# A row of 1/rms for 256 tokens: two small transfers by way of DRAM in place of a product with diagonals

## The chip, the cores and the metric

The kernel runs on one core of one Trainium2 chip. The metric is the device time of one execution in microseconds (us), lower is better. Five engines matter here: PE (TensorE, with its weight loads shown as PEld), DVE (VectorE), ACT (ScalarE), POOL (GpSimd) and SP (SyncE, which only issues transfers). Each works through its own list of instructions in order and waits on semaphores for the others; transfers run on 16 DMA engines.

## The reference

A decoder trunk of two layers on 256 tokens of width 1024, all float32. Each layer norms its input, multiplies it with a wide input projection, runs two attention-like branches, and ends in an MLP. The part that the change touches is the first norm of a layer and what is scaled by it:

```python
def rmsnorm(x, gain):
    y = xf * lax.rsqrt(jnp.mean(xf * xf, axis=-1, keepdims=True) + NORM_EPS)
    return (y * gain).astype(x.dtype)

for l in range(DEPTH):                       # DEPTH = 2
    h = rmsnorm(x, g_mix[l])
    proj = jnp.matmul(h, w_in[l])            # 256 x 1024 times 1024 x 9216
    q_r, k_r, v_r, g_r, q_s, k_s, v_s, gate_a, gate_b = jnp.split(proj, splits, axis=-1)
    ...                                      # rotary + retention, stick-breaking attention, gates
    x = x + jnp.matmul(merged, w_out[l])
    h = rmsnorm(x, g_mlp[l])
    x = x + jnp.matmul(jnp.square(jax.nn.relu(jnp.matmul(h, w_up[l]))), w_down[l])
return rmsnorm(x, g_final)
```

## The kernel before, in words

**The product stream.** All weights go through one stream of units (512 x 512 floats, 1 MB each, loaded on SP's queue, L62). Each unit is cut into two halves of 2 x 128 rows. `_split` (L67) turns a half into a high part `whi` (a cast on ACT, L75) and a low part `wlo` (a subtraction on DVE, L78), and PE multiplies the high and low parts with high and low parts of the activations. `raw` has 3 buffers, `whi` and `wlo` have 4 each, and `ahead` (L86) splits three halves ahead of the one that PE takes. A call of `cols512` (L368) does four halves, that is 512 output columns; after each half it calls a `tick` function, in which work of other kinds is slipped in. `half_T` and `half_W` give the product with the columns on the partitions and the tokens along the free axis; `half_N` the other way round.

**The norm.** The gain is multiplied into the activations ahead of the product, the factor 1/rms of each token only behind it. `Norm.rstd` (L299) adds the sums of squares on DVE and calls `rstd_col` (L230), which ends in a power on POOL (L235) and gives a column `r`: 128 partitions x 2, one value per token. That column serves the products whose tokens lie on partitions. Where the tokens lie along the free axis (the q of the stick-breaking branch, and both rotary tables), the same 256 values are needed as a row on all 128 partitions: `rb`, 128 x 256.

**How the row is made before.** `diagonals` (L238) scales the identity with the two columns of `r` on DVE (two instructions, tile `dg`); `rstd_rows` (L246) multiplies a matrix of ones with `dg` on PE (tile `bc`, in a PSUM bank of pool psA) and copies the bank to `rb` on DVE.

**Where it stands.** `norm_tick` (L420) runs after each of the first eight halves of a layer. Halves 0 to 3 make the first 512 columns of q, halves 4 to 7 the second. The column `r` and the diagonals come at tick 3 in layer 0 and tick 4 in layer 1, the product of the row at tick 5 with the scaled tables `cr` and `sr` (L441, L442), and `evac` at tick 6: it multiplies the first 512 columns of q with `rb` (L460), splits them, and so gives back their PSUM banks. In layer 0 `columns(1)` follows: a small transposition of the second gains on PE (tile `gps`, also a bank of psA), copied by ACT into `gcol` (L191). A scheduler puts the instructions of each engine in order from these places, so an instruction can stand some places ahead of or behind where it is written; only those in `keep_in_program_order` stay as written.

**Banks.** psA has four banks, given out in turn. Halves 8 to 11 (the first 512 columns of k) need all four, so in layer 0 they need the banks of the first q columns and of `gps` free.

Of the kernel before, what the change touches and what calls it, by code (L numbers as in the profile page):

```python
# [11 lines left out]
F32 = mybir.dt.float32  # L12
# [3 lines left out]
ALU = mybir.AluOpType  # L16
PSUM = bass.MemoryType.PSUM

P = 128
D = 1024  # L20
S = 256
# [79 lines left out]
def kernel(ctx, tc, x, w_in, p_ret, p_sb, w_out, w_up, w_down, g_mix, g_mlp, g_final,  # L101
                      c_sq, c_tab, c_decay, out):
    nc = tc.nc
# [4 lines left out]
    lo_pool = ctx.enter_context(tc.tile_pool(name="lo", bufs=4))  # L108
    wk = ctx.enter_context(tc.tile_pool(name="wk", bufs=2))
    small = ctx.enter_context(tc.tile_pool(name="small", bufs=2))  # L110
    psA = ctx.enter_context(tc.tile_pool(name="psA", bufs=4, space=PSUM))
    psB = ctx.enter_context(tc.tile_pool(name="psB", bufs=4, space=PSUM))

# [29 lines left out]
    ident = const.tile([P, P], F32, name="ident")  # L143
# [19 lines left out]
    tri_f, ones = cst[:, 0, :], cst[:, 1, :]  # L163
# [3 lines left out]
    def load_constants():  # L167
        nc.sync.dma_start(out=gn[1], in_=g_mlp.rearrange("l (k p) -> (l k) p", p=P))
        nc.sync.dma_start(out=cst, in_=c_sq[:, 1:3, :])
        nc.sync.dma_start(out=tab, in_=c_tab)  # L170
        nc.sync.dma_start(out=dec, in_=c_decay)
# [15 lines left out]
    def columns(i):  # L187

        gps = psA.tile([P, 512], F32, tag="a", name="gps")
        nc.tensor.transpose(gps[:, :16], gn[i], ident[0:16, 0:16])  # L190
        nc.scalar.copy(out=gcol[:, 16 * i:16 * i + 16], in_=gps[:, :16])  # L191
# [43 lines left out]
        nc.gpsimd.tensor_tensor(out=r[:, :n], in0=v[:, :n], in1=half[:, :n], op=ALU.pow)  # L235
        return r

    def diagonals(r):  # L238

        dg = wk.tile([P, 768], F32, tag="z", name="dg")[:, 0:S]  # L240
        for t in range(2):
            tc.keep_in_program_order(
                nc.vector.tensor_scalar(dg[:, t * P:(t + 1) * P], ident, r[:, t:t + 1], None, ALU.mult))
        return dg

    def rstd_rows(dg):  # L246

        bc = psA.tile([P, 512], F32, tag="a", name="bc")
        nc.tensor.matmul(bc[:, :S], lhsT=ones, rhs=dg, start=True, stop=True)
        rb = wk.tile([P, S], F32, tag="rb", name="rb", bufs=1)  # L250
        nc.vector.tensor_copy(out=rb, in_=bc[:, :S])
        return rb

    class Norm:
# [160 lines left out]
    def mix(l, norm):  # L415
        h = norm.h
        state = {"n": 0}


        def norm_tick():  # L420
            state["n"] += 1
            if l == 0 and state["n"] == 1:
                load_constants()
            if l == 0 and state["n"] <= 3:
                for i in ((0,), (1, 2), (3,))[state["n"] - 1]:
                    tc.keep_in_program_order(norm.square(*divmod(i, 2)))
            if state["n"] == (3 if l == 0 else 4):
                state["rc"] = norm.rstd()
                state["dg"] = diagonals(state["rc"])
            if state["n"] == 4:  # L430
                if l == 0:
                    tc.keep_in_program_order(nc.vector.tensor_copy(out=trir, in_=tri_f))
                    tc.keep_in_program_order(nc.vector.tensor_copy(out=onesr, in_=ones))
            if state["n"] == 5:
                rc = state["rc"]
                rb = rstd_rows(state["dg"])
                rcs = small.tile([P, 2], F32, tag="rcs", name="rcs")
                nc.vector.tensor_scalar(rcs, rc[:, 0:2], P ** -0.5, None, ALU.mult)
                cr = wk.tile([P, S], F32, tag="cr", name="cr", bufs=1)
                sr = wk.tile([P, S], F32, tag="sr", name="sr", bufs=1)  # L440
                nc.vector.tensor_tensor(out=cr, in0=tab[:, 0, :], in1=rb, op=ALU.mult)  # L441
                nc.vector.tensor_tensor(out=sr, in0=tab[:, 1, :], in1=rb, op=ALU.mult)  # L442
                state.update(rb=rb, rcs=rcs, cr=cr, sr=sr)
            if state["n"] == 6:
                state["evac"]()
                if l == 0:
                    columns(1)
# [29 lines left out]
        if l == 0:  # L477
            pairs0 = cols512(half_T, h, norm_tick)
        else:
            pairs0 = halves(cols512(half_W, h, norm_tick, four(psA, "a")))  # L480
        state["evac"] = lambda: evac_q(0, pairs0)
        evac_q(1, halves(cols512(half_W, h, norm_tick, four(psB, "b"))))
        rc, rb, rcs = state["rc"], state["rb"], state["rcs"]
        for c in range(2):
# [364 lines left out]
```

## Time and profile before

| | |
|---|---|
| Time, median of 3 runs | 905.8 us (905.64 to 905.99) |
| The profiled execution's own time | 906.1 us |
| Its span (first to last instruction) | 904.4 us |
| Granted TensorE clock | 1.00 throughout |
| PE busy | 896.4 us, 99% of the span |
| DVE busy | 616.3 us, 68% |
| ACT busy | 532.3 us, 59% |
| POOL busy | 12.2 us, 1% |
| 16 DMA engines, weight queue | 55.0% of the span, 161.89 MB |

How to read it: a busy share is an average over the whole span, so a small edit is read from the stage in which it stands. Layer 0's stage is the first 35 us of the span, layer 1's the stretch from 450 to 480 us. The chain that ended last tells which engine's work set the end; an idle time in a timeline stands in brackets with what ended it. Times within a timeline are microseconds from the span's start.

### The profile page before, as it was taken

To read this page: it belongs to the slowest core of one execution; us is meant where nothing else is said; L and a number is where in the kernel's file an instruction comes from. 1 tells how busy PE (TensorE), PEld (TensorE's weight loads), DVE (VectorE), ACT (ScalarE), POOL (GpSimd) and SP (SyncE) were. 2 spreads that over 40 slices of the span, in tenths; PEclk is the share of its full clock that TensorE was granted. 3 is DMA by queue.
4 is the path that set the end of the run, shared out by engine and by line. 5 is a ranking of instruction groups with operands and counts; after the bars stand their busy time and mean duration, and the time that the engine had idled before them with its cause. 6 is when DMAs were issued, how large, how long until landed. Compare 5 with 4: busy or idle time off the path is not lost.

```text
span 904.4 us, 11880 instructions
## 1 busy us (share of the span) xinstructions
PE 896.4 (99%) x4608; PEld 762.5 (84%) x4608; DVE 616.3 (68%) x829; ACT 532.3 (59%) x760; POOL 12.2 (1%) x20
## 2 busy tenths in 40 slices
PE   9999999999999999999999999999999999999997
PEld 7888888888888888888888888888888888888886
DVE  5865995775666666666676579857756666666665
ACT  5755688544456555555656566875444574646472
POOL 0000000000000000000000000000000000000000
PEclk9999999999999999999999999999999999999999
DMA  9755454545555655555555654544555655565641
GB/s 328 232 186 186 140 187 140 186 140 186 187 187 179 193 187 186 187 190 185 192 179 189 194 177 149 178 155 153 170 197 187 186 187 186 186 190 188 202 165 47
DMA packets 82151, 163.83 MB, mean 181 GB/s; under 512 B 2704, under 2 KB 3120, under 8 KB 82096
## 3 DMA queue, kind: packets, MB, share of 16 engines
q1 hardware_dynamic: 81488, 161.89, 55.0%
q10 hardware_dynamic: 608, 1.19, 0.4%
q8 instruction: 36, 0.59, 0.3%
q14 instruction: 19, 0.16, 0.1%
HBM read 162.02 MB, written 1.05 MB: 180 GB/s over the span
## 4 chain that ended last, share of the span: by engine, by line
PE 99%; DMA 1%; ACT 0%; DVE 0%; POOLq 0%; issue 0%; ACTq 0%
PE pa L356 18%; PE pa L358 18%; PE pa L357 18%; PE pb L333 12%; PE pa L333 11%; PE pb L337 6%; PE pa L337 5%; PE tp L225 1%; PE pa L319 1%; PE rop L636 1%; PE pb L356 1%; PE pb L358 1%; PE pb L357 1%; PE op L562 1%; PE z L518 1%; DMA x<-in_x_dram 1%
## 5 line engine op out<-in xcount | busy, mean ns | idle before, releaser
L78 DVE TENSOR_TENSOR wlo<-raw,whi 128x1024 fp32r<-128x1024 f32 (+1 forms) x306 | 371.5, 1216 | 234.4 <-ACT whi L75 231.2
L75 ACT CAST whi<-raw 128x1024 fp32r<-128x1024 f32 (+1 forms) x305 | 318.3, 1046 | 296.6 <-PE pa L357 195.4
L333 PE MATMUL pb<-h,whi 128*128 128x512 f32 x448 | 141.2, 396 | 0.0
L333 PE MATMUL pa<-h,whi 128*128 128x512 f32 x416 | 131.0, 396 | 0.0
L356 PE MATMUL pa<-whi,h 128*128 128x512 f32 x288 | 114.3, 397 | 0.0
L358 PE MATMUL pa<-wlo,h 128*128 128x512 f32 x288 | 112.4, 390 | 0.0
L357 PE MATMUL pa<-whi,h 128*128 128x512 f32 x288 | 112.2, 390 | 0.0
L337 PEld LDWEIGHTS pb<-h,wlo 128*128 128x128 f32 x448 | 84.1, 188 | 20.0 <-DVE wlo L78 0.2
L337 PEld LDWEIGHTS pa<-h,wlo 128*128 128x128 f32 x416 | 78.1, 188 | 18.4
L356 PE MATMUL pa<-whi,up 128*128 128x512 f32 x240 | 93.5, 390 | 0.0
L357 PE MATMUL pa<-whi,up 128*128 128x512 f32 x240 | 93.4, 389 | 0.0
L358 PE MATMUL pa<-wlo,up 128*128 128x512 f32 x240 | 93.4, 389 | 0.0
L337 PE MATMUL pb<-h,wlo 128*128 128x256 f32 x448 | 88.0, 278 | 0.0
L337 PE MATMUL pa<-h,wlo 128*128 128x256 f32 x416 | 81.8, 278 | 0.0
L333 PEld LDWEIGHTS pb<-h,whi 128*128 128x128 f32 x448 | 68.5, 189 | 0.3
L333 PEld LDWEIGHTS pa<-h,whi 128*128 128x128 f32 x416 | 64.0, 189 | 0.7
L358 PEld LDWEIGHTS pa<-wlo,h 128*128 128x128 f32 x288 | 54.1, 188 | 11.8
L357 PEld LDWEIGHTS pa<-whi,h 128*128 128x128 f32 x288 | 54.2, 188 | 10.2
L356 PEld LDWEIGHTS pa<-whi,h 128*128 128x128 f32 x288 | 54.2, 188 | 10.1
L358 PEld LDWEIGHTS pa<-wlo,up 128*128 128x128 f32 x240 | 45.0, 188 | 9.4
L356 PEld LDWEIGHTS pa<-whi,up 128*128 128x128 f32 x240 | 45.0, 188 | 9.0
L357 PEld LDWEIGHTS pa<-whi,up 128*128 128x128 f32 x240 | 45.0, 188 | 9.0
(177 smaller groups left out, 1139.8 us busy)
## 6 DMA issues: line engine op xcount, KB each, us to landing
raw<-in_w_in_dram SPq DMA_DIRECT2D x62, 1024.0 KB, 5.2
raw<-in_w_up_dram SPq DMA_DIRECT2D x32, 1024.0 KB, 5.4
raw<-in_w_down_dram SPq DMA_DIRECT2D x32, 1024.0 KB, 5.0
raw<-in_p_sb_dram SPq DMA_DIRECT2D x8, 1024.0 KB, 5.1
raw<-in_p_ret_dram SPq DMA_DIRECT2D x8, 1024.0 KB, 5.1
raw<-in_w_out_dram SPq DMA_DIRECT2D x8, 1024.0 KB, 5.1
raw<-in_w_in_dram SPq DMA_DIRECT2D x3, 512.0 KB, 6.7
x<-in_x_dram SPq DMA_DIRECT2D x3, 256.0 KB, 6.6
```

The costliest lines, as they stand in the source:

```text
L75: m = self.nc.scalar.copy(out=hi[:, sl], in_=src[:, sl])
L78: m = self.nc.vector.tensor_tensor(out=lo[:, sl], in0=src[:, sl], in1=hi[:, sl].bitcast(F32), op=ALU.subtract)
L225: m = nc.tensor.transpose(tp[:, a * S + t * P:a * S + (t + 1) * P], src(t)[:, f:f + P], ident)
L319: nc.tensor.matmul(banks[o // 2][:, (o % 2) * S:(o % 2 + 1) * S], lhsT=w[:, kk, o * P:(o + 1) * P], rhs=a, start=first and kk == 0 and n = ...
L333: nc.tensor.matmul(banks[o], lhsT=whi[:, kk, o * P:(o + 1) * P], rhs=a.rearrange("p a b -> p (a b)"), start=first and kk == 0, stop=False, ...
L337: nc.tensor.matmul(banks[o][:, S:2 * S], lhsT=wlo[:, kk, o * P:(o + 1) * P], rhs=act[(k0 + kk) // 2][:, kk, 0, :], start=False, stop=last ...
L356: nc.tensor.matmul(banks[t], lhsT=ahi, rhs=whi[:, kk, :], start=st, stop=False)
L357: nc.tensor.matmul(banks[t], lhsT=alo, rhs=whi[:, kk, :], start=False, stop=False)
L358: nc.tensor.matmul(banks[t], lhsT=ahi, rhs=wlo[:, kk, :], start=False, stop=sp)
L518: nc.tensor.matmul(z0[:, j * S:(j + 1) * S], lhsT=k0[c][:, a, r + j, :], rhs=part(qs, 2 * i + j, b), start=(n == 0 and j == 0), stop=(n == ...
L562: nc.tensor.matmul(op[:, o:o + S], lhsT=v0[c][:, a, e], rhs=wp[:, j, b, :], start=(n == 0 and j == 0), stop=False, skip_group_check=True)
L636: nc.tensor.matmul(op[:, o:o + S], lhsT=sc[:, i, a:b], rhs=vr[hd][:, t, j, :], start=(n == 0 and a == 0), stop=(n == 2 and t == 1), skip_g ...
```

## The change

The diagonals, the product with ones and the copy from PSUM go away. In their place POOL issues two transfers as soon as it has made `r`: the 128 x 2 column is written to a 1 KB buffer in DRAM (token order, so each of the 256 values is a run of its own), and that buffer is read back into `rb` once for each of the 128 partitions. The second waits for the first. `cr`, `sr` and `evac` move to tick 7 in layer 0 and tick 8 in layer 1.

```diff
+    dram = ctx.enter_context(tc.tile_pool(name="dram", bufs=2, space=bass.MemoryType.DRAM))
...
-    def diagonals(r):
-        dg = wk.tile([P, 768], F32, tag="z", name="dg")[:, 0:S]
-        for t in range(2):
-            tc.keep_in_program_order(
-                nc.vector.tensor_scalar(dg[:, t * P:(t + 1) * P], ident, r[:, t:t + 1], None, ALU.mult))
-        return dg
-    def rstd_rows(dg):
-        bc = psA.tile([P, 512], F32, tag="a", name="bc")
-        nc.tensor.matmul(bc[:, :S], lhsT=ones, rhs=dg, start=True, stop=True)
+    def rows(r):
+        row = dram.tile([2, P], F32, tag="row", name="row")
+        nc.gpsimd.dma_start(out=row.rearrange("t p -> p t"), in_=r[:, 0:2])
         rb = wk.tile([P, S], F32, tag="rb", name="rb", bufs=1)
-        nc.vector.tensor_copy(out=rb, in_=bc[:, :S])
+        nc.gpsimd.dma_start(out=rb, in_=row.rearrange("t p -> (t p)").partition_broadcast(P))
         return rb
...
             if state["n"] == (3 if l == 0 else 4):
                 state["rc"] = norm.rstd()
-                state["dg"] = diagonals(state["rc"])
+                state["rb"] = rows(state["rc"])
...
-            if state["n"] == 5:
-                rc = state["rc"]
-                rb = rstd_rows(state["dg"])
+            if state["n"] == (7 if l == 0 else 8):
+                rc, rb = state["rc"], state["rb"]
...
-            if state["n"] == 6:
                 state["evac"]()
                 if l == 0:
                     columns(1)
```

How the order moves, at three places. In the rows, the number behind `whi` or `wlo` is the half of the stream (0 to 151 are layer 0, 152 onwards layer 1, so 157 is half 5 of layer 1); the number behind the underscore only names a buffer. A DMA in a wait's name is a transfer, DMASW one that POOL issued.

DVE in layer 0, from the end of the norm to the scaled tables, before:

```order
L243 TENSOR_SCALAR dg_295<-ident_83,r_293 128x128 [waits Pool_49]
L243 TENSOR_SCALAR dg_295<-ident_83,r_293 128x128
L78 TENSOR_TENSOR wlo4_301<-raw2_101,whi4_300 128x1024 [waits DMAHW2_49,Activation_49]
L78 TENSOR_TENSOR wlo5_305<-raw2_101,whi5_304 128x1024 [waits Activation_49]
L78 TENSOR_TENSOR wlo6_311<-raw3_207,whi6_310 128x1024 [waits DMAHW7_49,Activation_49]
L432 CAST trir_160<-cst_103 128x128 [waits DMAHW4_49]
L433 CAST onesr_161<-cst_103 128x128
L438 TENSOR_SCALAR rcs_368<-r_293 128x2
L78 TENSOR_TENSOR wlo7_345<-raw3_207,whi7_344 128x1024 [waits Activation_49]
L251 COPY rb_366<-bc_364 128x256 [waits PE_49]
L78 TENSOR_TENSOR wlo8_377<-raw4_298,whi8_376 128x1024 [waits DMAHW0_49,Activation_49]
L441 TENSOR_TENSOR cr_370<-tab_104,rb_366 128x256 [waits DMAHW5_49,DVE_49]
```

and after:

```order
L78 TENSOR_TENSOR wlo4_304<-raw2_103,whi4_303 128x1024 [waits DMAHW2_49,Activation_49]
L78 TENSOR_TENSOR wlo5_308<-raw2_103,whi5_307 128x1024 [waits Activation_49]
L78 TENSOR_TENSOR wlo6_314<-raw3_209,whi6_313 128x1024 [waits DMAHW7_49,Activation_49]
L425 CAST trir_162<-cst_105 128x128 [waits DMAHW4_49]
L426 CAST onesr_163<-cst_105 128x128
L430 TENSOR_SCALAR rcs_409<-r_295 128x2 [waits Pool_49]
L78 TENSOR_TENSOR wlo7_348<-raw3_209,whi7_347 128x1024 [waits Activation_49]
L433 TENSOR_TENSOR cr_411<-tab_106,rb_299 128x256 [waits DMAHW5_49,DMASW1_49]
L434 TENSOR_TENSOR sr_412<-tab_106,rb_299 128x256
L451 TENSOR_TENSOR u_415<-pa_177,rb_299 128x512
L451 TENSOR_TENSOR u_420<-pa_178,rb_299 128x512 [waits PE_49]
L78 TENSOR_TENSOR wlo8_370<-raw4_301,whi8_369 128x1024 [waits DMAHW0_49,PE_49,Activation_49]
```

What moved: DVE no longer waits for POOL ahead of wlo4, so wlo4 follows the norm's last small instruction at once; and wlo8, which stood ahead of `cr`, now stands behind `cr`, `sr` and both `u`, all of which wait for the second transfer.

ACT in layer 0, around the first q columns, before:

```order
L75 CAST whi8_376<-raw4_298 128x1024 [waits DMAHW0_49,DVE_49,PE_49]
L75 CAST whi9_409<-raw4_298 128x1024 [waits DVE_49,PE_49]
L197 CAST qs_162<-u_396 128x2x256 [waits DVE_49]
L463 COPY q1_166<-u_396 128x256
L197 CAST qs_163<-u_401 128x2x256 [waits DVE_49]
L463 COPY q1_166<-u_401 128x256
L191 COPY gcol_114<-gps_406 128x16 [waits PE_49]
L75 CAST whi10_431<-raw5_308 128x1024 [waits DMAHW1_49,PE_49,Activation_49]
```

and after:

```order
L75 CAST whi8_369<-raw4_301 128x1024 [waits DMAHW0_49,DVE_49,PE_49]
L198 CAST qs_164<-u_415 128x2x256 [waits DVE_49]
L454 COPY q1_168<-u_415 128x256
L198 CAST qs_165<-u_420 128x2x256 [waits DVE_49]
L454 COPY q1_168<-u_420 128x256
L75 CAST whi9_389<-raw4_301 128x1024 [waits PE_49,Activation_49]
L75 CAST whi10_430<-raw5_311 128x1024 [waits DMAHW1_49,PE_49,Activation_49]
L192 COPY gcol_116<-gps_425 128x16 [waits PE_49]
```

What moved: the cast of whi9 now stands behind the four instructions that wait for DVE's `u`, and the copy that frees the bank of `gps` behind whi9 and whi10.

DVE in layer 1, from the norm's column onwards, before:

```order
L243 TENSOR_SCALAR dg_4177<-ident_83,r_4175 128x128 [waits Pool_49]
L243 TENSOR_SCALAR dg_4177<-ident_83,r_4175 128x128
L438 TENSOR_SCALAR rcs_4222<-r_4175 128x2
L78 TENSOR_TENSOR wlo156_4110<-raw78_3994,whi156_4109 128x1024 [waits DMAHW2_49,PE_49,Activation_49]
L216 SCALAR_TENSOR_TENSOR h_3880<-tp_4089,gcol_114,h_3880 128x256 [waits PE_49,Activation_49]
L216 SCALAR_TENSOR_TENSOR h_3880<-tp_4089,gcol_114,h_3880 128x256
L216 SCALAR_TENSOR_TENSOR h_3881<-tp_4098,gcol_114,h_3881 128x256 [waits PE_49,Activation_49]
L216 SCALAR_TENSOR_TENSOR h_3881<-tp_4098,gcol_114,h_3881 128x256
L78 TENSOR_TENSOR wlo157_4130<-raw78_3994,whi157_4129 128x1024 [waits PE_49,Activation_49]
L78 TENSOR_TENSOR wlo158_4152<-raw79_4028,whi158_4151 128x1024 [waits DMAHW3_49,PE_49,Activation_49]
```

and after:

```order
L430 TENSOR_SCALAR rcs_4282<-r_4174 128x2 [waits Pool_49]
L78 TENSOR_TENSOR wlo156_4109<-raw78_3993,whi156_4108 128x1024 [waits DMAHW2_49,PE_49,Activation_49]
L217 SCALAR_TENSOR_TENSOR h_3879<-tp_4088,gcol_116,h_3879 128x256 [waits PE_49,Activation_49]
L217 SCALAR_TENSOR_TENSOR h_3879<-tp_4088,gcol_116,h_3879 128x256
L217 SCALAR_TENSOR_TENSOR h_3880<-tp_4097,gcol_116,h_3880 128x256 [waits PE_49,Activation_49]
L217 SCALAR_TENSOR_TENSOR h_3880<-tp_4097,gcol_116,h_3880 128x256
L433 TENSOR_TENSOR cr_4284<-tab_106,rb_4178 128x256 [waits DMASW3_49]
L78 TENSOR_TENSOR wlo157_4129<-raw78_3993,whi157_4128 128x1024 [waits PE_49,Activation_49]
L434 TENSOR_TENSOR sr_4285<-tab_106,rb_4178 128x256
L78 TENSOR_TENSOR wlo158_4151<-raw79_4027,whi158_4150 128x1024 [waits DMAHW3_49,PE_49,Activation_49]
```

What moved: `cr`, which before came behind wlo160 (half 8), now stands ahead of wlo157 (half 5), and with it the wait for the second transfer.

## Rows read from the trace of the kernel before

**Rows 1.** The page's busy times of the engines (us, share of the span, instructions), its line of the weights' queue (packets, MB, the time that its packets took as a share of the span of 16 engines), the first line of the chain that ended last (share of the span by engine), and one group of the page's costliest (busy us, mean ns of one, then the idle time before them and what ended it).
```profile
PE 896.4 (99%) x4608; PEld 762.5 (84%) x4608; DVE 616.3 (68%) x829; ACT 532.3 (59%) x760; POOL 12.2 (1%) x20
...
q1 hardware_dynamic: 81488, 161.89, 55.0%
...
PE 99%; DMA 1%; ACT 0%; DVE 0%; POOLq 0%; issue 0%; ACTq 0%
...
L75 ACT CAST whi<-raw 128x1024 fp32r<-128x1024 f32 (+1 forms) x305 | 318.3, 1046 | 296.6 <-PE pa L357 195.4
```

**Rows 2.** The chain that ended last, in order of time, around the product `bc` in layer 0 and in layer 1: start, us, what.
```profile
22.43 0.23 PE pb L337 x2
22.66 0.43 PE bc L249 x2
23.09 0.46 PE pb L333 x2
...
468.44 0.43 PE bc L249 x2
468.87 0.46 PE pb L333 x2
```

**Rows 3.** Timeline of POOL: start, us, instruction, in brackets the idle time before it and what ended it. The first and the third row are the norms that the change is about.
```profile
17.66 0.70 POOL L235 TENSOR_TENSOR r<-v,half 128x2 f32<-128x2 f32 x1 [16.31 <-DVE v L233]
169.14 1.61 POOL L235 TENSOR_TENSOR r<-v,half 128x2 f32<-128x2 f32 x1 [150.78 <-DVE v L233]
...
456.25 0.69 POOL L235 TENSOR_TENSOR r<-v,half 128x2 f32<-128x2 f32 x1 [177.31 <-DVE v L233]
```

**Rows 4.** Timeline of DVE, layer 0 from the norm to the evacuation of q, and one row at 169 us.
```profile
17.41 0.17 DVE L233 TENSOR_SCALAR v<-ms 128x2 f32<-128x2 f32 x1
18.40 0.48 DVE L243 TENSOR_SCALAR dg<-ident,r 128x128 f32<-128x128 f32 x2 [0.82 <-POOL r L235]
18.80 2.35 DVE L78 TENSOR_TENSOR wlo<-raw,whi 128x1024 fp32r<-128x1024 f32 x2
...
24.55 1.22 DVE L78 TENSOR_TENSOR wlo<-raw,whi 128x1024 fp32r<-128x1024 f32 x1
...
27.16 0.42 DVE L441 TENSOR_TENSOR cr<-tab,rb 128x256 f32<-128x256 f32 x1
27.49 0.42 DVE L442 TENSOR_TENSOR sr<-tab,rb 128x256 f32<-128x256 f32 x1
27.83 1.28 DVE L460 TENSOR_TENSOR u<-pa,rb 128x512 f32<-128x512 f32 x2
29.02 1.21 DVE L78 TENSOR_TENSOR wlo<-raw,whi 128x1024 fp32r<-128x1024 f32 x1
...
168.97 1.22 DVE L78 TENSOR_TENSOR wlo<-raw,whi 128x1024 fp32r<-128x1024 f32 x1
```

**Rows 5.** Timeline of ACT in layer 0: the casts of whi4 and whi5, of whi8 and whi9, and the work on the first q columns up to the copy of `gcol`.
```profile
16.50 2.00 ACT L75 CAST whi<-raw 128x1024 fp32r<-128x1024 f32 x2
...
24.67 2.06 ACT L75 CAST whi<-raw 128x1024 fp32r<-128x1024 f32 x2 [0.68 <-DVE rcs L438]
28.54 0.62 ACT L197 CAST qs<-u 128x512 fp32r<-128x512 f32 x1 [1.81 <-DVE u L460]
...
30.20 0.16 ACT L191 COPY gcol<-gps 128x16 f32<-128x16 f32 x1
```

**Rows 6.** Timeline of PE: the first and the fourth run of half 8 in layer 0, and the start of half 5 in layer 1 (behind `bc`).
```profile
31.67 0.63 PE L333 MATMUL pa<-h,whi 128*128 128x512 f32 x2
...
33.76 0.63 PE L333 MATMUL pa<-h,whi 128*128 128x512 f32 x2
...
468.28 0.60 PE L249 MATMUL bc<-dg,cst 128*128 128x256 f32 x2
```

**Rows 7.** Timeline of DVE in layer 1: the last instructions ahead of the place where `cr` now stands, and wlo157.
```profile
458.58 1.65 DVE L216 SCALAR_TENSOR_TENSOR h<-tp,gcol,h 128x256 fp32r<-128x256 f32 x4
461.02 1.22 DVE L78 TENSOR_TENSOR wlo<-raw,whi 128x1024 fp32r<-128x1024 f32 x1 [0.79 <-ACT whi L75]
```

**Rows 8.** Transfers: tile written and read, issuing queue, count, KB each, median us from issue to landing. The ACT queue carries only the loads of `gn`, `x` and `gfin` and stores at the end; the SP queue carries the weights.
```profile
out_dram<-ob SPq DMA_DIRECT2D x2, 320.0 KB, 2.5
...
out_dram<-ob ACTq DMA_DIRECT2D x2, 192.0 KB, 2.7
x<-in_x_dram ACTq DMA_DIRECT2D x1, 256.0 KB, 4.9
...
cst<-in_sq_dram SPq DMA_DIRECT2D x1, 128.0 KB, 7.9
gn<-in_g_mix_dram ACTq DMA_DIRECT2D x1, 8.0 KB, 2.7
gn<-in_g_mlp_dram SPq DMA_DIRECT2D x1, 8.0 KB, 8.2
```

**Rows 9.** Stretches of time: busy us of each engine (and instructions), granted clock, mean busy share of the 16 DMA engines, GB/s. The first two lie in the time of the two transfers in layer 0, the others in layer 1.
```profile
20.00:22.00 2.00, 2.00 (x13) 1.75 (x12) 1.15 (x2) 0.01 (x1) 0.00 (x0) 1.00 0.97 361
...
24.00:26.00 2.00, 2.00 (x14) 1.62 (x12) 2.00 (x6) 1.33 (x2) 0.00 (x0) 1.00 0.86 329
457.00:459.00 2.00, 2.00 (x14) 1.74 (x13) 2.00 (x6) 1.76 (x5) 0.00 (x0) 1.00 0.88 270
...
461.00:463.00 2.00, 2.00 (x14) 1.73 (x13) 1.22 (x1) 0.29 (x1) 0.00 (x0) 1.00 0.04 8
```

More of the change, by code (lines that the diff above doesn't have):

```diff
@@ L442, in norm_tick @@
                 nc.vector.tensor_tensor(out=sr, in0=tab[:, 1, :], in1=rb, op=ALU.mult)
-                state.update(rb=rb, rcs=rcs, cr=cr, sr=sr)
-            if state["n"] == 6:
+                state.update(rcs=rcs, cr=cr, sr=sr)
                 state["evac"]()
```

## The prediction

> **What bounds the kernel now.** I read the shares first. PE is busy for 896.4 of 904.4 us, and the chain that ended last runs on PE for 99% of the span [rows 1]. What feeds PE is not the limit: the casts of the weights on ACT idle for 296.6 us, and most of that ends when PE gives a buffer back [rows 1]. So time goes away only where PE has less to do, and comes on only where PE is made to wait. Next I read the two places where the row of 1/rms is made. The product `bc` lies on the chain itself: 0.43 us in layer 0, 0.43 us in layer 1, with products of the weight stream right before and behind [rows 2]. The rest of the page is then of no interest; what matters is how late `rb` may come before PE notices, and how late it will come.
>
> One thing on size: 0.2% of the time is 1.8 us, about what a measurement of this kernel can tell from no change.
>
> **The change, part by part.**
>
> *Taken away from PE.* Two places of 0.43 us: 0.86 us [rows 2]. The small transposition `gps` of layer 0 is only moved by a half, so it costs what it did.
>
> *Taken away from DVE.* Two diagonals (0.48 us) and a copy from PSUM per layer. I count this as nothing, since DVE is 68% busy [rows 1] and PE is covered by the three halves that are split ahead.
>
> *A wait that goes, and what is late next.* In layer 0 DVE stood for 0.82 us until POOL had `r`, then made the diagonals, then wlo4 [rows 4]. Now wlo4 follows the norm's last small instruction, which ends at 17.58, since whi4, the first of two casts that take 2.00 us from 16.50, is then done [rows 5]. So wlo4 will run just when POOL takes its power at 17.66, which was 0.70 us long [rows 3]. The trace has one case of this: at 169.14 the same power began under a wlo that ran from 168.97 to 170.19, and took 1.61 us [rows 3, 4]. I therefore put `r` of layer 0 at 17.66 + 1.61 = 19.3 instead of 18.4. The Trainium skill states this rule (SBUF — State Buffer, Who interferes with whom): a DVE instruction with two inputs in SBUF and a GpSimd instruction that reads SBUF block each other for the whole instruction; the 1.61 us against 0.70 agree. In layer 1 DVE still waits for `r` (`rcs` stands first), so `r` is there at 456.25 + 0.69 = 456.9 [rows 3].
>
> *How late `rb` may come, layer 0.* DVE's `cr` waits for the second transfer; behind it on DVE stand `sr`, two `u`, wlo8, and on ACT, through `u`, four instructions on q, whi9, whi10 and the copy of `gcol`. Who waits for those: PE at half 8, which began at 31.67 and now begins 0.43 earlier, at 31.24 [rows 2, 6]. It has two prices.
> First, wlo8 is needed after two products of together 0.46 us [rows 2], at 31.70. From the start of `cr` to the end of a wlo behind it took 30.23 - 27.16 = 3.07 us [rows 4]. So `cr` may start at 28.6.
> Second, the fourth run of half 8 needs the bank of `gps`, at 33.76 - 0.43 = 33.33 [rows 6]. From `cr` to the first q cast is 28.54 - 27.16 = 1.38, the four on q take 30.20 - 28.54 = 1.66, two casts 2.06, the copy 0.16 [rows 4, 5]: 5.26 us. So `cr` may start at 28.1. That is the tighter one: 28.1 - 19.3 = 8.8 us for both transfers. DVE comes to `cr` at about 24.55 + 1.22 = 25.8 [rows 4], so a transfer done by then costs nothing at all.
>
> *How late, layer 1.* `cr` stands right behind the four `h`, which ended at 460.2 [rows 7]; behind it stands wlo157. PE needs that 0.46 us into half 5, whose place began at 468.28 with `bc` [rows 6]: at 468.74. Less wlo157 (1.22) and the step from `cr` to the next instruction (0.33) [rows 4, 7], `cr` may start at 467.2: 467.2 - 456.9 = 10.3 us for both transfers.
>
> *The two transfers.* No row shows a transfer that POOL issues, nor one to DRAM that another waits for, so I bound it. Below: 2.5 us, the store with empty queues [rows 8]; twice, since the second waits for the first, 5.0 us. Above: 8.2 us, the 8 KB load of `gn` behind weights on SP's queue [rows 8]; twice, 16.4 us. Nearest are transfers on a queue of their own: 8 KB at the very start 2.7 us, 256 KB beside a full weight queue 4.9 us [rows 8]. I take the middle of these two, 3.8 us each, 7.6 us for both. A second way agrees: a weight packet costs 0.55 x 904.4 x 16 / 81488 = 0.098 us of one engine [rows 1]; the column goes as 256 packets, 16 per engine, the row as 128, 8 per engine; with 2.7 us each that is 2.7 + 1.6 + 2.7 + 0.8 = 7.8 us.
> The Trainium skill (DMA: Bandwidth & Descriptors, Rules for kernel authors) speaks against such a first transfer: a strided last dimension goes as one descriptor per element. The same page (Anatomy of one DMA) gives about 2.0 us fixed for a transfer issued on POOL; by that, as an estimate, both would be done after 4.0 us and the sum would be the same.
> With 7.6 us `rb` lands at 26.9 in layer 0, 1.2 us ahead of its limit though the DMA engines are 97% and 86% busy there, and at 464.5 in layer 1, 2.7 us ahead, where they fall to 4% [rows 9]. DVE waits 1.1 us and about 4 us; PE does not notice.
>
> *Sum.* The profiled execution took 906.1 us: 906.1 - 0.86 = 905.2. The median of the runs lies 0.3 us below that execution, so I forecast **905.0 us**.
>
> **The rivals.**
>
> *The transfers are somewhat slow in layer 0.* The 4.9 us row holds for each, or up to 6 us: `rb` at 29.1 to 31.3, PE waits 1.0 to 3.2 us at half 8, layer 1 stays inside its limit or passes it by 1.7 at the far end. For it: both run while the DMA engines are full [rows 9]. Against: the 4.9 us moved 256 KB. 905.9 to 908.1 us, more only at the far end; 14%.
>
> *DVE holds up POOL's transfers too, not only the power.* Issuing costs POOL work, and DVE runs wlo5 and wlo7 in that time. At the price of 1.61 - 0.69 = 0.92 us each [rows 3], `rb` lands at 28.7, 0.6 late: 905.6 us. For it: the 1.61 us. Against: that was an instruction that reads SBUF. By the Trainium skill (SBUF — State Buffer, Who interferes with whom) it is DVE's casts and copies that hold descriptor writing, and a TENSOR_TENSOR was not seen to; no run here shows it yet. 8%.
>
> *Slower: each transfer takes as long as a small load did behind weights.* One mechanism: a small transfer gets through only when the weight packets ahead of it are done, 8.2 us each [rows 8]. Then `rb` lands at 19.3 + 16.4 = 35.7 and 473.3; PE waits 7.6 us at half 8 in layer 0 and 6.1 us at half 5 in layer 1: 905.0 + 13.7 = 918.7 us. It decides from 8.8 us for the pair on; 0.2% is passed at 11.5 us for the pair. For it: two rows of about 8 us [rows 8]. Against: those stood on SP's own queue; POOL's has nothing else in it. 13%.
>
> *The product was free.* If PE's next products had to wait for whi or wlo anyway, nothing is gained and nothing lost: 905.8 us. Against it stand the casts that wait for PE [rows 1]. 7%.
>
> *Faster by more.* Only if the whole opening of layer 0 tightens through the earlier wlo4; PE has 8.0 us without work in all [rows 1], most of it before its first weights. About 903.7 us; 3%.
>
> **How the numbers follow.** The forecast has 55%. The range runs from 904.4 (the lowest run, 905.64, less 0.86 and another 0.4 for scatter) to 907.6: it holds the forecast, the free product, the held issue and the slow layer 0 but for its far end (3 of its 14%). Left out are 13% + 3% + 3% = 19%. Slower by over 0.2%: 13% + 3% = 16%. Faster by over 0.2%: 3%. Within: 81%.
>
> **What would show it.** Right: no `bc` in the chain; products of the weight stream back to back where it stood; no idle PE between 30 and 35 us nor around 468 us; the power of layer 0 about 1.6 us long; both transfers together under 8.8 us from the end of the power in layer 0, under 10.3 in layer 1; DVE idle before `cr`. Wrong: PE idle at the first or fourth run of half 8, released by wlo8 or `gcol`; or PE idle at half 5 of layer 1, released by wlo157; the length of that idle time is then the loss, one for one. And if `r` comes at 18.4, the step on the blocked power is wrong, without harm to the sum.

## The result, and the profile after

The change is slower. Its median is 918.41 us (917.75 to 920.41, 4 runs) against 905.89 us of the kernel before (4 runs on the same chip): ratio 1.0137, 95% interval 1.0125 to 1.0149, 12.5 us. I had forecast 905.0 us, and 904.4 to 907.6 as the range. The profiled execution of the changed kernel took 917.75 us, its span is 916.0 us, 11.6 us more than before. (In after, the power stands in line 236, the store in 242, the load in 244, the wide products in 326 and 330.)

The page after, busy times (us, share of the span, instructions) and the first line of the chain that ended last:

```profile
PE 897.8 (98%) x4604; PEld 762.8 (83%) x4604; DVE 614.8 (67%) x823; ACT 531.5 (58%) x760; POOL 16.1 (2%) x24
...
PE 93%; DMA 4%; DVE 1%; issue 1%; ACT 0%; POOL 0%; POOLq 0%; DVEq 0%; ACTq 0%
```

Beside [rows 1], PE is busy for 1.4 us more (below: a lower clock), and the chain runs on it for 93% of the span instead of 99%. The chain in order of time (start, us, what) shows what came between, in layer 0 and in layer 1, where before there were only products with `bc` among them [rows 2]:

```profile
19.86 10.76 DMA row<-r
30.91 5.80 DMA rb<-row
37.50 1.20 DVE u L451 x2
38.70 1.14 DVE wlo L78
39.88 0.79 PE pa L330 x2
...
466.38 8.71 DMA row<-r
475.13 0.51 issue
475.65 3.20 DMA rb<-row
479.22 1.23 DVE wlo L78
480.49 0.50 PE pb L330 x2
```

It is the path that the prediction drew, from the power (POOL's timeline below) by two transfers to a split and to PE, with two durations that are not what it took: the store 10.76 and 8.71 us, the load 5.80 and 3.20 us, against 3.8 us each. What PE waited for (line, releaser, us in total, times, longest):

```profile
PE pa L330 <- DVE wlo L78: 7.3, 1, 7.3
PE pb L330 <- DVE wlo L78: 2.4, 1, 2.4
...
PE pa L326 <- ACT whi L75: 0.3, 1, 0.3
```

These are half 8 of layer 0 and half 5 of layer 1, the two places named. To see what else layer 0 lost, stretches around the wait (us; busy time and instructions of PE, PE's weight loads, DVE, ACT, POOL; granted clock; DMA share; GB/s):

```profile
36.70:39.80 3.10, 0.00 (x0) 0.00 (x0) 3.06 (x6) 1.67 (x5) 0.00 (x0) 0.50 0.00 0
39.80:43.00 3.20, 3.12 (x11) 2.73 (x12) 3.20 (x5) 2.59 (x6) 0.00 (x0) 0.53 0.00 0
43.00:46.00 3.00, 3.00 (x19) 2.60 (x19) 2.83 (x6) 2.27 (x5) 0.00 (x0) 1.00 0.84 273
```

Towards the end of the idle time the granted clock fell to 0.50, the lower of its two levels (1.2 of 2.4 GHz), and PE's next 3.2 us ran at 0.53: 3.20 x 0.47 = 1.5 us more.

To add up a layer I use POOL's power of the norm and that of the first head behind it. Timeline of POOL after, and the row of before that [rows 3] lack:

```profile
17.84 1.71 POOL L236 TENSOR_TENSOR r<-v,half 128x2 f32<-128x2 f32 x1 [16.48 <-DVE v L234]
178.32 1.62 POOL L236 TENSOR_TENSOR r<-v,half 128x2 f32<-128x2 f32 x1 [146.82 <-DVE v L234]
465.40 0.69 POOL L236 TENSOR_TENSOR r<-v,half 128x2 f32<-128x2 f32 x1 [177.31 <-DVE v L234]
625.98 1.61 POOL L236 TENSOR_TENSOR r<-v,half 128x2 f32<-128x2 f32 x1 [149.76 <-DVE v L234]
```

```profile
614.61 1.53 POOL L235 TENSOR_TENSOR r<-v,half 128x2 f32<-128x2 f32 x1 [157.67 <-DVE v L233]
```

Layer 0: 178.32 - 17.84 = 160.48 us against 169.14 - 17.66 = 151.48: 9.00 more. Of these 7.3 + 0.3 are waits, 1.5 the clock, -0.43 the product; 0.3 stays over. Layer 1: 160.58 against 158.36: 2.22 more, which is 2.4 - 0.43 and 0.2 over. Together 11.2 of the 11.6 us; the rest is a start 0.2 us later and 0.2 us at the end.

So the place of the loss is plain. What the runs had to tell is why a store of 1 KB takes 9 to 11 us. Two things in the trace of after spoke against my slower rival's reason (weight packets ahead of it) as the whole of it. In layer 1 a weight load does run ahead of the store, and the store's last packet, at 469.6 us, runs together with that load's last one; but no weight load is under way from then on, and the store still lands only at 475.1, 5.5 us later (one line of POOL's queue between 468 and 470 us: packets, MB, share; and a stretch behind it, columns as above):

```profile
q0 software_dynamic: 32, 0.00, 1.6%
```

```profile
471.00:473.00 2.00, 2.00 (x13) 1.74 (x12) 0.00 (x0) 1.14 (x2) 0.00 (x0) 1.00 0.00 0
```

And in layer 0 it is the weights that suffer, with two loads of 1 MB under way:

```profile
25.00:26.00 1.00, 1.00 (x7) 0.87 (x6) 1.00 (x4) 0.00 (x0) 0.00 (x0) 1.00 0.29 27
26.00:27.00 1.00, 1.00 (x8) 0.91 (x7) 0.34 (x1) 0.00 (x0) 0.00 (x0) 1.00 0.00 0
...
28.00:29.00 1.00, 1.00 (x6) 0.78 (x5) 0.00 (x0) 0.00 (x0) 0.00 (x0) 1.00 0.58 135
```

The load issued at 16.7 us, 3 us ahead of the store, took 13.9 us to land (8.0 before); whi8, which needs it, began at 30.76 instead of 24.67 [rows 5]:

```profile
L62 SPq DMA_DIRECT2D raw<-in_w_in_dram x1: 378/378/378, 16.7 to 16.7; - x1
...
DMA to landing us min/median/max: 13.9/13.9/13.9
```

### The profile page after: what moved, and what is told of

Same layout as the page of the kernel before. It is cut to its first block, busy times and chain, and to the rows that moved or that the text cites. A ratio compares the mean times of both kernels' runs of the same rounds, so it can differ in the third digit from the quotient of the medians.

```text
span 916.0 us, 11869 instructions
## 1 busy us (share of the span) xinstructions
PE 897.8 (98%) x4604; PEld 762.8 (83%) x4604; DVE 614.8 (67%) x823; ACT 531.5 (58%) x760; POOL 16.1 (2%) x24
## 4 chain that ended last, share of the span: by engine, by line
PE 93%; DMA 4%; DVE 1%; issue 1%; ACT 0%; POOL 0%; POOLq 0%; DVEq 0%; ACTq 0%
PE pa L349 18%; PE pa L350 18%; PE pa L351 18%; PE pb L326 10%; PE pa L326 10%; PE pb L330 5%; PE pa L330 5%; DMA row<-r 2%; PE tp L226 1%; DMA rb<-row 1%; PE rop L627 1%; DMA raw<-in_w_in_dram 1%; PE pb L349 1%; PE pb L351 1%; PE pb L350 1%; PE op L553 1%
```

## The experiments

Three theories of the long transfers. **Small pieces to DRAM**: the store goes as 256 pieces of 4 bytes, and these are slow whatever issues them. **POOL's queue**: the queue is slow whatever it carries. **Weight packets ahead**: the rival on record. The table has all timed runs. "Store" is the time from the first store's issue to the load's issue; "layer" is the stretch from power to power less that of before (151.48 and 158.36 us); each with layer 0 / layer 1, in us.

| kernel | median us | ratio to before (95%) | store | PE waits | layer |
|---|---|---|---|---|---|
| the change | 918.41 | 1.0137 (1.0125 to 1.0149) | 11.1 / 9.3 | 7.6 / 2.4 | +9.00 / +2.22 |
| store on ACT's queue | 921.34 | 1.0161 (1.0144 to 1.0178) | 11.1 / 9.0 | 6.7 / 2.8 | +9.87 / +5.88 |
| layer 1 only | 909.69 | 1.0041 (1.0026 to 1.0056) | none / 9.3 | 0 / 3.0 | 0.00 / +2.79 |
| row in SBUF | 913.46 | 1.0079 (1.0064 to 1.0094) | 7.0 / 4.9 | 4.6 / 0 | +7.19 / -0.52 |
| pairs of 8 bytes | 910.45 | 1.0048 (1.0033 to 1.0063) | 6.1 / 5.7 | 2.4 / 0 | +2.61 / -0.51 |
| turned, 128 bytes | 908.15 | 1.0019 (1.0011 to 1.0028) | 5.7 / 4.3 | 1.5 / 0 | +2.02 / -0.45 |
| splits ahead | 920.18 | 1.0142 (1.0127 to 1.0157) | 12.0 / 10.7 | 9.0 / 2.1 | +11.58 / +2.71 |
| turned, work ahead | 905.50 | 0.9991 (0.9982 to 0.9999) | 5.7 / 4.2 | 0 / 0 | -0.45 / -0.46 |
| turned, layer 1 only | 905.74 | 0.9997 (0.9988 to 1.0006) | none / 4.3 | 0 / 0 | 0.00 / -0.45 |

**1. A probe of the forms.** To the kernel before, stores of a head's 1/rms are added that nobody reads:

```
+ hd 0: dma_start(out=a.rearrange("t p -> p t"), in_=r[:, 0:2])           # run:  a [2, P]
+ hd 1: dma_start(out=a, in_=r[:, 0:2])                                   # pair: a [P, 2]
+ hd 2: dma_start(out=a[:, :, 0].rearrange("t p -> p t"), in_=r[:, 0:2])  # line: a [2, P, 16]
+ hd 3: dma_start(out=z[0:1, 0:P], in_=r[:, 0:1])                         # sbuf
```

> The kernel before, with eight extra stores of a head's 1/rms that nobody waits for: in four heads of layer 0 on POOL's queue, in the same four heads of layer 1 on ACT's queue. Forms: run = 256 pieces of 4 bytes to 1 KB of DRAM (the form of the change), pair = 128 pieces of 8 bytes to DRAM, line = 256 pieces of 4 bytes, each in a 64-byte line of its own, sbuf = 128 pieces of 4 bytes into one partition of SBUF. Theory 'small pieces to DRAM' (the store itself is slow, about 5 us of it after its last packet): run takes 8.5 to 11 us from issue to landing on both queues, sbuf 2.5 to 4 us on both, pair and line lie between. Theory 'POOL's queue' : all four forms take 8 to 11 us on POOL and 2.5 to 4 us on ACT. Theory 'weight packets ahead' (my slower rival): the time goes with the share of busy DMA engines at the place, not with form or queue, and is under 4 us wherever that share is near 0. Time 905.5 to 907, since nothing waits for these stores.

Transfers of the probe in layer 0 on POOL's queue, then in layer 1 on ACT's (tile, queue, count, KB, us from issue to landing):

```profile
parun<-r POOLq DMA_DIRECT2D x1, 1.0 KB, 10.7
pbpair<-r POOLq DMA_DIRECT2D x1, 1.0 KB, 6.3
pcline<-r POOLq DMA_DIRECT2D x1, 1.0 KB, 4.2
pdsbuf<-r POOLq DMA_DIRECT2D x1, 0.5 KB, 2.0
...
qarun<-r ACTq DMA_DIRECT2D x1, 1.0 KB, 11.7
qbpair<-r ACTq DMA_DIRECT2D x1, 1.0 KB, 3.7
qcline<-r ACTq DMA_DIRECT2D x1, 1.0 KB, 5.0
qdsbuf<-r ACTq DMA_DIRECT2D x1, 0.5 KB, 2.0
```

The form sets the time, not the queue. And it is not the number of pieces: run and line are 256 pieces of 4 bytes each, 11 us against 4 to 5; what differs is how they lie in DRAM, one right behind the other in the run, 64 bytes apart in line. The one execution took 908.55 us, above the 905.5 to 907 that I expected. PE's listed waits name none of these stores, but POOL's power of the next head stood until the run had landed, at 183.11 and 629.28 us, so it was wrong that nothing waits for them. And 1.4 us of the time added lie ahead of the first store (152.84 us from the norm's power to the first head's, against 151.48); their cause stays open.

**2. The probe with places and queues exchanged.** Run moves from the first of the four heads to the last, ACT's queue serves layer 0, POOL's layer 1, and in place of sbuf stands gap, 256 pieces of 4 bytes, one every 32 bytes:

```
- if hd == 0:   (run)        + if hd == 3:
- if hd == 1:   (pair)       + if hd == 2:
- if hd == 2:   (line)       + if hd == 1:
- if hd == 3:   (sbuf)       + if hd == 0:   a [2, P, 8], a[:, :, 0] written   (gap)
- queue = gpsimd if l == 0 else scalar      + queue = scalar if l == 0 else gpsimd
```

> The probe again with the places and the queues exchanged (the run of 4-byte pieces now in the last of the four heads instead of the first; ACT's queue in layer 0, POOL's in layer 1), and in the first head, in place of the store into SBUF, a gap form: 256 pieces of 4 bytes to DRAM, one every 32 bytes. If the form sets the time: run 8.5 to 12 us again, line 4 to 5, pair 3.5 to 6.5, gap between line and run. If the place did it: the first head's store takes 10 to 12 us whatever its form, and the run in the last head 2 to 4 us.

```profile
pdgap<-r ACTq DMA_DIRECT2D x1, 1.0 KB, 5.0
pcline<-r ACTq DMA_DIRECT2D x1, 1.0 KB, 1.6
pbpair<-r ACTq DMA_DIRECT2D x1, 1.0 KB, 4.1
parun<-r ACTq DMA_DIRECT2D x1, 1.0 KB, 9.6
```

In layer 1 the same order reads 4.8, 2.0, 4.2 and 9.1 us. The run is slow in every place and on either queue; line came out faster than I expected, and gap as slow as line in the first probe. The one execution took 906.54 us, against 906.14 of the kernel before.

The packets in the traces part each store's time in two. On ACT's queue the run (between 203.0 and 203.4 us) and line (182.3 to 182.7) look alike:

```profile
q10 hardware_dynamic: 272, 0.00, 36.5%
...
q10 hardware_dynamic: 272, 0.00, 37.0%
```

From the issue to the store's last packet it took 1.1 to 1.6 us where no weight load was under way, 1.7 to 4.7 us beside one, whatever the form; that is nearly the whole difference between line's 1.6 and 2.0 us here and its 4.2 and 5.0 in the first probe, and as far as this part goes my rival was right. From the last packet to the landing the form decides: the run 6.4, 7.0, 8.5 and 7.6 us in the four places, the pairs 0.5 to 3.3, gap 0.6 and 0.7, line 0.5 to 0.6, sbuf 0.6. The change's own store took 4.9 + 5.9 us in layer 0 and 3.2 + 5.5 in layer 1. So pieces of 4 bytes are slow when packed, and not when one stands every 32 bytes; at which distance that begins, and whether the pairs gain by their size or by their number, these runs do not tell.

The weight loads near the stores tell the second half: the one issued 3 us behind the run, and the last one well ahead of it (issue; landing in us):

```profile
L62 SPq DMA_DIRECT2D raw<-in_p_ret_dram x1: 367/367/367, 205.1 to 205.1; - x1
...
DMA to landing us min/median/max: 11.7/11.7/11.7
```

```profile
L62 SPq DMA_DIRECT2D raw<-in_p_ret_dram x1: 368/368/368, 196.6 to 196.6; - x1
...
DMA to landing us min/median/max: 4.9/4.9/4.9
```

1 MB took 11.7 us instead of 4.9 (5.8 for the same load in the kernel before); beside gap, line and pair in this probe the loads kept to 4.9 to 5.5 us. So behind the store's last packet the causes run the other way than in my rival: the small writes hold up the weights.

The Trainium skill (DMA: Bandwidth & Descriptors, Specifications) says that below 512 bytes a DMA engine reads, modifies and writes. A run of small pieces being slow agrees, 9.1 to 11.7 us here; but by size alone line would be as slow, and it took 1.6 to 5.0 us. The same page (Anatomy of one DMA) has most of a transfer's fixed 2.0 us spent on the receipt of the write, longest where the target is HBM. The run's wait of 6.4 to 8.5 us behind its last packet agrees in kind; as a constant the 2.0 us does not hold for it. The store into SBUF took 2.0 us in all, but with only 0.6 of it behind the last packet. What goes on inside DRAM or the engines no run here shows.

**3. The store on ACT's queue.** `- nc.gpsimd.dma_start(out=row...)` `+ nc.scalar.dma_start(out=row...)`

> The change with one edit: the store of the column is issued on ACT's queue, the load of the row stays on POOL. 'Small pieces to DRAM': the store still takes 8.5 to 11 us, PE still waits 6 to 9 us in layer 0 and 1.5 to 3.5 us in layer 1, 916 to 920 us. 'POOL's queue': the store takes 2.5 to 4 us, the row is there by 28.5 and 466, PE waits for nothing, 905 to 906 us. 'Weight packets ahead': as small pieces in layer 0, no wait in layer 1: about 914 us.

The store is as slow as from POOL, so POOL's queue is out as the reason. The median is 921.34 us, a little above my range: the load took 7.89 us in layer 0, and in layer 1 the wait of 2.6 us was here followed by some 6 us at the lower clock (0.63 from 480 to 484 us, 0.51 from 484 to 488), where the change's 2.4 us at the same place left it at 1.00.

**4. Transfers in layer 1 only.** Layer 0 keeps the diagonals, the product and the order of before:

```
- state["rb"] = rows(state["rc"])
+ if l == 0:  state["dg"] = diagonals(state["rc"])      # and rstd_rows at half 5
+ else:       state["rb"] = rows(state["rc"])
- if state["n"] == (7 if l == 0 else 8):
+ if state["n"] == (5 if l == 0 else 8):
```

> Transfers in layer 1 alone; layer 0 keeps diagonals and product. If PE's waits are the loss, one for one: layer 1 loses its 2.4 us of PE waiting for wlo157 and saves 0.43 us, with no loss of granted clock: 907.9 us (907.4 to 908.5), PE idle 2 to 3 us at half 5 of layer 1. If layer 1's wait came only from weights that ran late behind layer 0's: 905.5 us, no idle PE in layer 1. If the moved order costs by itself, beside the waits: 909 us or more.

Layer 0 is back to 151.48 us to the hundredth, layer 1 alone costs 2.79 us, 3.0 of waiting less 0.43 and 0.2 over. So the two losses are separate, and this one counts one for one. The median is 1.2 us above my range, where I had put the third case, a moved order that costs by itself. The trace does not show that: this store took 9.0 and the load 3.8 us, each somewhat more than in the change, and run 10, which has the same places and a shorter store, loses nothing. The four runs scatter over 1.7 us; that the transfers scatter is likely, but only one of the four has a trace.

**5. The row in SBUF.**

```
- row = dram.tile([2, P], F32, tag="row", name="row")
- nc.gpsimd.dma_start(out=row.rearrange("t p -> p t"), in_=r[:, 0:2])
+ row = wk.tile([P, 768], F32, tag="z", name="row")[0:1, 0:S]
+ for t in range(2):
+     nc.gpsimd.dma_start(out=row[:, t * P:(t + 1) * P], in_=r[:, t:t + 1])
- rb <- row.rearrange("t p -> (t p)").partition_broadcast(P)
+ rb <- row[:, None, :].to_broadcast([1, P, S])
```

> The change with the row in one partition of SBUF instead of DRAM: two stores on POOL's queue of 128 pieces of 4 bytes each, then the load of that row into all partitions, all on POOL's queue as in the change. 'Small pieces to DRAM': the stores land after 2.5 to 4 us, the load after 3 to 6 us, rb is there 6.5 to 9.5 us after r, PE waits 0 to 1 us in layer 0 and not in layer 1: 905 to 906.5 us. 'POOL's queue', or the number of pieces whatever their target: still 8 us or more for the stores, 915 to 920 us.

Half a hit. Each store took 3.7 to 5.7 us, half of the one to DRAM but not the 2.5 to 4 expected; and a load of 128 KB out of one partition took 6.6 and 6.7 us. Layer 1 has no wait any more and is 0.52 us shorter than before; layer 0 is 7.0 + 6.6 us behind the first issue and waits 4.6 us. The clock then cost more than the change's: PE ran at 0.50 from 36.6 to 42 us and at 0.84 to 44, 3.0 us; 4.6 - 0.43 + 3.0 = 7.2, the row of the table.

**6. Pairs of 8 bytes.**

```
- row = dram.tile([2, P], ...);  store out=row.rearrange("t p -> p t")
+ row = dram.tile([P, 2], ...);  store out=row
- in1=rb
+ in1=rb.rearrange("p (q t) -> p t q", t=2)     # cr, sr and u; each u now in two instructions
```

> The change with the row laid out in DRAM as pairs: the store goes as 128 pieces of 8 bytes (both 1/rms of a partition side by side) instead of 256 pieces of 4; the three readers of rb read it with a stride. 'Small pieces to DRAM': the store takes 6.3 us in layer 0 and 3.7 to 6.3 in layer 1 (the two pair rows of the probe), the load 5.8 and 3.2 as in the change; rb is there about 4 us after its limit in layer 0 and inside it in layer 1; PE waits 3 to 4.5 us once, and loses 1 to 2 us more at the lower granted clock: 908 to 911 us. 'Weight packets ahead' or a store whose time does not go by its pieces: as the change, 917 to 920 us.

The time is as expected, the waits a little under it: with half as many pieces, each twice as large, the load is issued 5 us sooner after the store in layer 0 and 3.5 in layer 1; 4.1 us over the kernel before are left of 12.5, with 2.4 us of waits in layer 0 (I had said 3 to 4.5) and none in layer 1.

**7. The column turned on DVE, pieces of 128 bytes.**

```
+ z = wk.tile([P, 768], F32, tag="z", name="turn");  nc.gpsimd.memset(z[:, 0:32], 0.0)
+ nc.vector.tensor_copy(out=z[:, 0:2], in_=r[:, 0:2])
+ nc.vector.transpose(out=z[:, 32:64], in_=z[:, 0:32])
- nc.gpsimd.dma_start(out=row.rearrange("t p -> p t"), in_=r[:, 0:2])
+ for t in range(2):
+     nc.gpsimd.dma_start(out=row[t:t + 1, :].rearrange("t (b i) -> (t b) i", i=32), in_=z[t:P:32, 32:64])
```

> The change with the column first turned on DVE in blocks of 32 x 32 (a copy of two columns and one transposition of 128x32, a memset of 32 columns on POOL ahead of them); then two stores on POOL's queue of four pieces of 128 bytes each, and the same load of the row from DRAM. All of the path by way of DRAM is kept, only the pieces grow. 'Small pieces to DRAM': both stores land within 3.5 us of the first issue, the load 3 to 6 us later, rb is inside its limits in both layers, PE does not wait, and what I forecast of the change comes true: 905.0 us (904.6 to 905.8), two places of 0.43 us less than before. 'Any store to DRAM that a load waits for is slow': 913 us or more. 'POOL's queue': 915 or more.

By way of the same DRAM and the same queue, with larger pieces, 1.8 us are left of 12.5. (Two things moved with the pieces: DVE waits for `r` again, to turn it, so the power of layer 0 took 0.70 us and not 1.71; and the scheduler put wlo8 between the two `u`.) What is left is layer 0's: store and load took 5.7 + 5.0 us there, not 3.5 + 3 to 6, and `cr` began 1.55 us behind the limit of 28.1 that the prediction worked out. What PE then waited for are the two prices that it named, wlo8 and the copy of `gcol`, 1.5 us together (DVE's timeline, then PE's waits):

```profile
29.65 0.42 DVE L438 TENSOR_TENSOR cr<-tab,rb 128x256 f32<-128x256 f32 x1 [4.64 <-DMA rb<-row]
```

```profile
PE pa L331 <- ACT gcol L192: 0.9, 1, 0.9
PE pa L335 <- DVE wlo L78: 0.6, 1, 0.6
```

The four runs of half 8 took 5.2 us instead of 2.8, so 0.9 us more went in gaps that the profile lists no wait for, and PE lost 2.4 us in all. Layer 1 gains its 0.45 us.

**8. The splits ahead of the wait.** The change's transfers, and more of the order of DVE and of ACT's casts pinned:

```
- if h < 5:  self.pin(m)
+ if h < 12 or 152 <= h < 164:  self.pin(m)      # at both places: the cast on ACT, the subtraction on DVE
- nc.vector.tensor_scalar(rcs, ...)
+ tc.keep_in_program_order(nc.vector.tensor_scalar(rcs, ...))     # likewise cr, sr, the first two u
```

> The change with the same transfers, but on DVE the splits wlo8 and wlo9 stand ahead of cr in layer 0, and wlo157 to wlo163 in layer 1. If PE's waits are all of the loss and only what stands behind cr on DVE makes them: no idle PE in layer 1 at half 5 (2.4 us less); in layer 0 wlo8 is no longer late, but half 8 then needs the banks that the two u free, behind cr, so 1 to 2 of the 7.3 us come back: 914 to 916 us. If the length of the transfers cost in another way (weights that run late because DMA is slowed): 917 us or more.

A miss on both sides of my first branch; the time is that of the second, weights that run late. In layer 0 PE now waits for the banks that `u` frees, 9.0 us, and not less than before, since store and load were longer still (12.0 us from issue to issue, then 8.2). In layer 1 no split stands behind `cr` any more, yet PE waits 2.1 us, for a cast of weights. The chain and the wait there:

```profile
474.02 13.90 DMA raw<-in_w_in_dram
...
489.36 1.23 DVE wlo L78
...
490.66 0.33 DVE cr L433
...
498.01 0.96 ACT whi L75
```

```profile
PE pa L326 <- ACT whi L75: 2.1, 1, 2.1
```

A weight load issued during the small store took 13.90 us. The wlo that needed it now stood ahead of `cr`, so `cr` began at 490.57, 4.2 us after the row had landed at 486.41; ACT's copies of q came late behind it, and the cast that PE waited for, pinned, came behind those. So this order did not hide the loss but let the weights add to it; whether another order could, with such a store, is not shown.

**9. Turned, with the work ahead.** Run 7 with run 8's pins (casts and subtractions only up to half 9, none in layer 1), and in layer 0 the first q columns copied out of PSUM on ACT after half 3:

```
+ banks0 = two_banks();  pairs0 = [wk.tile([P, 768], F32, tag="e", name="u")[:, 0:512] for _ in range(2)]
+ if state["n"] == 4 and l == 0:  nc.scalar.copy(out=u, in_=b) for both;  columns(1)
- if state["n"] == 7 and l == 0:  columns(1)
```

> The version that the runs so far point to. The turned column with its stores of 128-byte pieces and the load from DRAM; and in layer 0 the work that PE waited for is put ahead of the wait for the row: wlo8 and wlo9 ahead of cr on DVE, the copy of gcol and two copies of the first q columns out of PSUM ahead on ACT. If PE's waits (1.5 us in layer 0 with the turned column alone) come only from what stands behind cr, no product of layer 0 or 1 waits, and both places of 0.43 us are gained: 0.5 to 1.1 us less than the kernel before. If the row is so late that DVE can't catch up with the splits from half 10 on, PE waits 1 to 3 us there: same as before, or up to 2 us more.

No product of layers 0 or 1 waits for `rb` any more. Timeline of POOL:

```profile
17.55 0.70 POOL L236 TENSOR_TENSOR r<-v,half 128x2 f32<-128x2 f32 x1 [16.16 <-DVE v L234]
168.58 1.63 POOL L236 TENSOR_TENSOR r<-v,half 128x2 f32<-128x2 f32 x1 [29.77 <-DVE v L234]
455.66 0.69 POOL L236 TENSOR_TENSOR r<-v,half 128x2 f32<-128x2 f32 x1 [177.31 <-DVE v L234]
613.56 1.55 POOL L236 TENSOR_TENSOR r<-v,half 128x2 f32<-128x2 f32 x1 [151.72 <-DVE v L234]
```

151.03 and 157.90 us, 0.45 and 0.46 less than before: the sum of the prediction, 0.86 us, to a tenth. It is 0.9991 of the kernel before (0.9982 to 0.9999), 0.6 us, the only version whose interval lies below 1, and only just.

**10. Turned, layer 1 only.** Run 4 with run 7's `rows`: `- store out=row.rearrange("t p -> p t")` `+ memset, copy, transpose, two stores of z[t:P:32, 32:64]`.

> Layer 0 as in the kernel before (diagonals and product), layer 1 with the turned column and 128-byte pieces. Layer 1 has 10.3 us, and the pair took about 8.7 us there: no idle PE at half 5 of layer 1, 0.43 us less than the kernel before (0.2 to 0.7 less), against 3.7 us more with the store of 4-byte pieces. If the transfers of layer 1 scatter by more than 2 us, PE waits up to 1 us: 0.5 us more than before.

905.74 us: 0.45 us gained in layer 1, nothing lost in layer 0; the time itself can't be told from no change.

## Why the prediction was wrong

**The step that failed is "The two transfers"**: 3.8 us each. It was read from 8 KB and 256 KB transfers whose pieces are large, and even its bound from above, 8.2 us, is under the store's 10.76 and 8.71 us. The second way, by packets, agreed only because it rested on the same 2.7 us: ACT's queue lists 272 packets for the store (run 2) and POOL's 32, and over all runs 4.9 to 8.5 of the store's 8.4 to 11.7 us lie behind the last one. No row of the kernel before shows such a wait. The rule at hand (the Trainium skill, DMA: Bandwidth & Descriptors, Rules for kernel authors: a strided last dimension goes as one descriptor per element) was weighed by the fixed cost of a transfer and found harmless. Runs 1 and 2 show what it cost: the wait behind the last packet goes by how densely the pieces lie in DRAM. Run 7, where only 0.3 to 0.8 us lie behind the last packet, has most of the loss back.

**What it left out**: that a small store can slow the weights (13.9 us for a load of 8.0; whi8 6 us late, PE 0.3 us), and that the granted clock fell in an idle time of 7.3 us and stayed at 0.53 for the next 3.2 us (1.5 us). So "one for one" failed in layer 0, where 7.6 us of waiting stand against 9.0 + 0.43 us of loss; in layer 1 it held to 0.2 us.

**What held.** The power of layer 0 blocked by wlo4: 1.71 us, `r` ready at 19.55 (said 19.3). The limits, in place and nearly in size: the waits of the change are released by wlo at half 8 and half 5. Counted from each layer's power, `cr` began 2.5 us behind its limit in layer 1, and PE waited 2.4; in layer 0 it began 8.0 us behind the wlo8 limit of 28.6, and PE waited 7.6. That in run 7 a `cr` 1.55 us late made waits of 1.5 us is in part luck: the order there was another, and PE lost 2.4 us. The two places of 0.43 us on PE: 0.45 to 0.52 us per layer wherever no product waits (runs 5, 6, 7, 9, 10), which also answers "The product was free". With a shorter store alone (run 7) the forecast did not come true; with the work ahead as well (run 9) it did, 905.50 us.

**The rivals.** "Slower" named the sign, both places and, at 918.7 us, nearly the time; its 13% were too few. Its reason was right in part: beside weights the store's last packet came after 3.2 to 4.9 us instead of 1.1 to 1.6. But 5.5 to 5.9 us lie behind that packet, in layer 1 at a DMA share of 0.00, and its price of 8.2 us for either transfer was in truth 10.8 and 5.8, 8.7 and 3.2, so the agreement to 0.3 us is luck in part: it had 6.1 us of waiting in layer 1, where 2.4 came, and nothing for the clock. "DVE holds up POOL's transfers" did not show: POOL issued the store 0.3 us behind the power in both layers.

## What to carry to other kernels

A column that has to become a row is not a 1 KB transfer but 256 writes, and packed in DRAM these took 8.4 to 11.7 us in every run here; before trusting a duration from the trace, match the pieces, not the bytes. If the way by DRAM is wanted, turn the column on an engine first, and put everything that PE will need behind the wait ahead of it. And work out how late a result may come, as here: that part of the sum held to 0.1 us in layer 1 and 0.4 in layer 0 of the change, and it tells at once which durations decide.

## What the runs showed that I had not expected

Packed 4-byte writes to DRAM slowed the weight loads issued beside them: no packet at all for 1 us and 27 to 135 GB/s around it, with two weight loads under way, and 11.7 and 13.9 us for loads that took 5.8 and 8.0 in the kernel before. The same 4-byte pieces 32 or 64 bytes apart landed 0.5 to 0.7 us behind their last packet, and the loads beside them in the second probe took 4.9 to 5.5 us.

A load of 128 KB into all partitions took 3.2 to 8.2 us from 1 KB of DRAM, and 6.6 and 6.7 us from one partition of SBUF.

Idle times of PE of 2.4 and 3.0 us left the granted clock at 1.00 (the change and run 4, layer 1), one of 2.6 us was followed by some 6 us near 0.5 (run 3, layer 1): a short wait has two prices, and one trace does not tell which.
